# Block products on 12 instead of 8 of the 24 row tiles in the down projections of each FFN's first half

## The chip, the core and the metric

The kernel runs on one core of a Trainium2 chip. The core has five engines that work side by side and wait for each other by semaphores: TensorE (PE in the profile, its weight loads as PEld) multiplies matrices into the accumulators in PSUM; VectorE (DVE) and ScalarE (ACT) work on tiles in SBUF and PSUM; GpSimd (POOL) works on SBUF; SyncE (SP) issues most of the transfers from memory. Each engine takes its instructions in a fixed order. The metric is the device time of one execution in microseconds (us), as the median of a few runs.

## The reference

One decoder layer on 256 tokens of width 2048, all in float32:

```
def swiglu(x, w_gate, w_up, w_down):
    return (jax.nn.silu(x @ w_gate) * (x @ w_up)) @ w_down

x = layer_norm(alpha * x + 0.5 * swiglu(x, ffn1_w_gate, ffn1_w_up, ffn1_w_down), ln1_g, ln1_b)
p = x @ w_in
mix = concatenate([diff_attn_group(p[..., :ATTN_COLS], ...), rwkv7_group(p[..., ATTN_COLS:], ...)]) @ w_out
x = layer_norm(alpha * x + mix, ln2_g, ln2_b)
x = layer_norm(alpha * x + 0.5 * swiglu(x, ffn2_w_gate, ffn2_w_up, ffn2_w_down), ln3_g, ln3_b)
```

The gate and up weights are 2048 x 5632, the down weights 5632 x 2048. The change touches only the two FFNs.

## The kernel before

**Float32 by parts.** Each operand is split into a high part (rounded to a shorter format) and a low part (the rest). A product of a 128-token tile with a row tile of weights (128 x 512) is three matmuls, high by high, high by low and low by high: lines 151, 152 and 153 in `product`. For weights the split is made on the fly: `load` brings a pair of row tiles (a 512 KB transfer, line 131, issued by SP), `halves` makes the high part on ACT (line 141, "wh") and the low part on DVE (line 144, "wl") into one of `NW["ffn"]` = 7 buffer pairs, which are free again once PE has used them. The sections below call such a split pair of row tiles a half.

**Order.** The program is written as one stream and handed to a planner, which lays it out on a simulated time line and by that fixes the order of the instructions on each engine ahead of the run. On the chip each engine follows that order, whatever the real durations are.

**An FFN.** The 5632 hidden columns are done in two halves, of six and of five blocks of 512. For each block j, gate and up are computed over the 16 row tiles of x, then `up_done` makes h = 0.5 silu(gate) up, transposes it on PE, and splits it into tiles hT. After the blocks of a half the down projection runs over that half's h: 24 row tiles in the first half, 20 in the second, 2048 output columns as two calls of `two_blocks`, each with two column blocks of 512. In the first half `down_done` (line 472) loads a piece rc of the residual by ACT's queue, after a one-column copy by GpSimd into the same tile (line 476), and writes alpha times rc plus the accumulator into the SBUF tiles y (line 478). The second half adds into y and ends with the layer norm.

**Block products.** `two_blocks` (from line 206) computes two column blocks for both token tiles together. Over the first eight row tiles, `ks[:8]`, it treats the work as a 2x2 by 2x2 product (two token tiles, two groups of four row tiles, two column blocks) and uses the scheme with seven block products in place of eight. It needs:

- sums of the x (or h) blocks, made once by `combinations` into the tiles S[0] to S[3]: eight sums on DVE (line 379, through temporaries in buffer `y0`), then four cuts into high and low part, the copy on ACT (line 383) and the difference on DVE;
- four raw weight tiles r11, r12, r22, r21 of four row tiles each, out of four buffers of tag `r4`, and four differences of them on DVE in place (`minus`, line 222, 128 x 2048);
- copies and additions of partial accumulators (lines 235 to 255).

`seven` does one block product: two halves of two row tiles each, six matmuls for each half. The remaining row tiles, `ks[8:]`, are plain work: `later` puts them in a list (`tail`), and `late(n)` runs the next n steps of that list, each one half of weights used by both token tiles, 12 matmuls. The rest of the first column block runs in the second half of its own call, the rest of the second column block in the first half of the next call; `n = len(self.tail) // 4` steps stand between one block product and the next, and what is left stands at the end.

**Who waits for whom.** A half must have been loaded (SP and the DMA queues), cast (ACT) and subtracted (DVE) before PE may use it, and its buffer comes free only after PE. Buffers with the names y0 and y1 hold x at the start, then temporaries (`y0`), then y for the rest of the FFN. The S tiles of h replace those of x when the last gate and up block has used them; those of x are stored to memory (`sd`) and read back for the second half.

## Time and profile before

| what | value |
|---|---|
| runs | 1920.59, 1918.80, 1920.53 us (median 1920.53) |
| the profiled execution | 1918.89 us, of which its span 1917.1 us |
| mean granted clock of TensorE | 0.996 of full speed |
| moved by DMA | 381.73 MB, on average 199 GB/s |
| block differences, line 222 | 112, of 2284 ns on average |
| matmuls of block sums, lines 151 to 153 | 448 each |

A row of a waits view reads: engine, tile and line that waited, then what it waited for, then the total in us, the number of times, the longest. A row of a groups view reads: line, engine, operation, output <- inputs, shapes, count, then busy us and the mean of one in ns, then the idle time of the engine in front of them with what ended it. A row of a timeline reads: start, length in us, engine, line, operation, count of instructions merged. The span counts from the first to the last instruction; the time of a run has some 1.8 us around that.

### The profile page before, as it was taken

The page shows a single profiled execution, that of the slowest core. Times are in us where ns is not written, and L with a number is a line of the kernel's source. Part 1 is how long each engine was busy: PE and PEld are TensorE (multiplying, and loading weights), DVE is VectorE, ACT ScalarE, POOL GpSimd, SP SyncE. Part 2 cuts the span into 40 slices and gives each one's busy share as a digit, 9 for nine tenths or more (in the row PEclk, how much of TensorE's full clock was granted, in tenths as well). Part 3 has the DMA queues.
Part 4 walks back from the last instruction along what each step waited for, and adds up shares of the span by engine and source line. Part 5 has one row for each costly group of instructions (what it writes and reads, how often), then busy time and mean ns, then how long its engine had stood idle before and what let it go on. Part 6 is the DMA issues. An engine that isn't in the chain of part 4 may idle for free. (4 is left out here: it accounts for less than half of the span.)

```text
span 1917.1 us, 24935 instructions
## 1 busy us (share of the span) xinstructions
PE 1881.4 (98%) x9335; PEld 1547.7 (81%) x9335; DVE 1623.1 (85%) x1834; ACT 1093.9 (57%) x1376; POOL 74.9 (4%) x110
## 2 busy tenths in 40 slices
PE   8999999999999999999999999999999999999997
PEld 7888888888888878887778877788888888888886
DVE  8999987789999976776678886999999778999986
ACT  6656664566666536645565543566666545666651
POOL 0000101100000000000000000000000110000000
PEclk9999999999999999999999999999999999999999
DMA  9766676765667456555445645775566676566744
GB/s 312 246 201 217 185 239 220 233 212 200 216 213 228 143 172 201 167 159 160 139 132 146 188 135 165 257 255 191 197 214 227 208 245 211 198 205 212 223 159 134
DMA packets 207322, 381.73 MB, mean 199 GB/s; under 512 B 23531, under 2 KB 25649, under 8 KB 206945
## 3 DMA queue, kind: packets, MB, share of 16 engines
q1 hardware_dynamic: 182928, 350.53, 55.7%
q0 software_dynamic: 6832, 15.32, 3.0%
q10 hardware_dynamic: 17440, 14.29, 2.6%
q8 instruction: 73, 1.20, 0.3%
q14 instruction: 49, 0.39, 0.1%
HBM read 368.29 MB, written 11.80 MB: 198 GB/s over the span
## 5 line engine op out<-in xcount | busy, mean ns | idle before, releaser
L141 ACT CAST wh<-raw 128x1024 fp32r<-128x1024 f32 (+2 forms) x833 | 852.6, 1047 | 596.6 <-PE acc L153 365.9
L144 DVE TENSOR_TENSOR wl<-raw,wh 128x1024 fp32r<-128x1024 f32 (+2 forms) x833 | 983.3, 1213 | 207.7 <-ACT wh L141 203.7
L152 PE MATMUL acc<-wl,xh 128*128 128x512 f32 (+1 forms) x1552 | 604.6, 391 | 4.0 <-DVE wl L144 4.0
L153 PE MATMUL acc<-wh,xl 128*128 128x512 f32 (+1 forms) x1552 | 603.2, 390 | 0.5 <-DVE xl L90 0.4
L151 PE MATMUL acc<-wh,xh 128*128 128x512 f32 (+1 forms) x1552 | 597.8, 393 | 5.9 <-ACT xh L89 4.6
L151 PEld LDWEIGHTS acc<-wh,xh 128*128 128x128 f32 x1552 | 291.7, 188 | 69.3 <-ACT xh L89 6.2
L152 PEld LDWEIGHTS acc<-wl,xh 128*128 128x128 f32 x1552 | 292.0, 188 | 63.6 <-DVE wl L144 5.4
L153 PEld LDWEIGHTS acc<-wh,xl 128*128 128x128 f32 x1552 | 292.0, 188 | 61.8 <-DVE xl L90 2.0
L222 DVE TENSOR_TENSOR raw<-raw,raw 128x2048 f32<-128x2048 f32 x112 | 255.8, 2284 | 1.0 <-DMA raw<-in_ffn_w_gate_dram 0.5
L152 PE MATMUL acc<-wl,hh 128*128 128x512 f32 x544 | 212.0, 390 | 0.0
L153 PE MATMUL acc<-wh,hh 128*128 128x512 f32 x544 | 211.4, 389 | 0.0
L151 PE MATMUL acc<-wh,hh 128*128 128x512 f32 x544 | 210.9, 390 | 0.0
L151 PE MATMUL acc<-wh,s 128*128 128x512 f32 x448 | 174.9, 390 | 1.0 <-ACT acc L248 1.0
L153 PE MATMUL acc<-wh,s 128*128 128x512 f32 x448 | 174.6, 390 | 0.0
L152 PE MATMUL acc<-wl,s 128*128 128x512 f32 x448 | 174.4, 389 | 0.0
L151 PEld LDWEIGHTS acc<-wh,hh 128*128 128x128 f32 x544 | 102.1, 188 | 21.7 <-ACT wh L141 0.4
L152 PEld LDWEIGHTS acc<-wl,hh 128*128 128x128 f32 x544 | 102.2, 188 | 21.1
L153 PEld LDWEIGHTS acc<-wh,hh 128*128 128x128 f32 x544 | 102.1, 188 | 20.9
L151 PEld LDWEIGHTS acc<-wh,s 128*128 128x128 f32 x448 | 84.1, 188 | 19.0 <-ACT acc L248 1.5
L153 PEld LDWEIGHTS acc<-wh,s 128*128 128x128 f32 x448 | 84.1, 188 | 17.5
L152 PEld LDWEIGHTS acc<-wl,s 128*128 128x128 f32 x448 | 84.1, 188 | 17.4
L235 ACT COPY acc<-acc 128x512 f32<-128x512 f32 x28 | 16.0, 571 | 51.5 <-PE acc L153 47.7
(264 smaller groups left out, 1100.0 us busy)
## 6 DMA issues: line engine op xcount, KB each, us to landing
raw<-in_ffn_w_up_dram SPq DMA_DIRECT2D x176, 512.0 KB, 5.3
raw<-in_ffn_w_down_dram SPq DMA_DIRECT2D x176, 512.0 KB, 5.4
raw<-in_ffn_w_gate_dram SPq DMA_DIRECT2D x175, 512.0 KB, 4.5
raw<-in_w_in_dram SPq DMA_DIRECT2D x96, 512.0 KB, 3.7
raw<-in_w_out_dram SPq DMA_DIRECT2D x32, 512.0 KB, 4.1
sd<-s POOLq DMA_DIRECT2D x16, 256.0 KB, 4.1
s<-sd POOLq DMA_DIRECT2D x16, 256.0 KB, 5.1
xs<-y ACTq DMA_DIRECT2D x16, 256.0 KB, 3.0
```

The source lines that it names most:

```text
L141: SC.copy(out=wh[:, c, :w], in_=raw[:, c, :w])
L144: self.cut = V.tensor_tensor(out=wl[:, c, :w], in0=raw[:, c, :w], in1=wh[:, c, :w].bitcast(F32), op=ALU.subtract).ins
L151: T.matmul(a, hi, wh[:, j, :w], start=first and j == 0, stop=False, skip_group_check=True)
L152: T.matmul(a, hi, wl[:, j, :w], start=False, stop=False, skip_group_check=True)
L153: i = T.matmul(a, lo, wh[:, j, :w], start=False, stop=last and j == 1, skip_group_check=True)
L222: V.tensor_tensor(out=out, in0=x, in1=y, op=ALU.subtract)
L235: SC.copy(out=u, in_=a)
```

## The change

In the first half of each FFN the down calls use block products for the first 12 row tiles instead of eight, so two groups of six; the remaining 12 are plain. The gate and up blocks and the down calls of the second half keep eight.

- The block sums of h for the two extra row tiles of each group come from h block 2. `half_tiles` makes them after the fourth gate and up block (j = 3): `combinations` on 128 x 256 pieces, with the eight sums on GpSimd (`by=G`), the cuts on ACT and DVE as before, the temporaries in `y0` and the results, S[4] to S[7], in `y1`.
- The extra raw weights (two row tiles each, one transfer of 512 KB) lie in the buffers of the seventh half (wh6, wl6) and in `y0`: `more_raws`. So these calls, and the last gate and up block in front of them, have six buffers for halves (`spare`). The differences are made on both parts, and `seven` runs three halves.
- With y0 and y1 taken, y can't be in SBUF during the first half. `down_done` now computes into rc and stores it to a tile `ys` in memory by ACT's queue; y is read back by GpSimd's queue ahead of the second block of the second half.

```diff
-        def two_blocks(self, cols, ks, x, comb, done, strict=False):
+        def two_blocks(self, cols, ks, x, comb, done, strict=False, extra=None, spare=0):
             assert not self.pend
-            self.buffers(NW["ffn"], LAG["ffn"])
+            self.buffers(NW["ffn"] - spare, LAG["ffn"])
...
-            def own(src, k, c):
-                return self.load(src, row + k, c, n=4)
+            done_rows = 8
+            if extra is not None:
+                done_rows = 12
+                more = dict(zip(("11", "12", "22", "21"), extra()))
+
+            def own(src, k, c, name):
+                r = [self.load(src, row + k, c, n=4)]
+                if extra is not None:
+                    t = more[name]
+                    self.loaded = nc.sync.dma_start(out=t, in_=src[(row + 8 + k // 2) * P:(row + 10 + k // 2) * P, c:c + NB].rearrange("(k p) n -> p k n", p=P)).ins
+                    r.append(t)
+                return r
 
             def minus(out, x, y):
-                V.tensor_tensor(out=out, in0=x, in1=y, op=ALU.subtract)
+                for o, a, b in zip(out, x, y):
+                    V.tensor_tensor(out=o, in0=a, in1=b, op=ALU.subtract)
 
             def seven(acc, lhs, raw, first=False, last=False):
-                for i in range(2):
-                    self.product(acc, lambda j: lhs(2 * i + j), *self.halves(raw[:, 2 * i:2 * i + 2]), first and i == 0, last and i == 1)
+                parts = [raw[0][:, 0:2], raw[0][:, 2:4]] + raw[1:]
+                for i, r in enumerate(parts):
+                    self.product(acc, lambda j: lhs(2 * i + j), *self.halves(r), first and i == 0, last and i + 1 == len(parts))
...
-            self.later(s0, c0, ks[8:], x, (a, w), lambda t, acc: done(0, t, acc), False)
+            self.later(s0, c0, ks[done_rows:], x, (a, w), lambda t, acc: done(0, t, acc), False)
...
-        def combinations(x, tmp, after=None):
-            def add(out, x, y, op=ALU.add):
+        def combinations(x, tmp, after=None, own=None):
+            def add(out, x, y, op=ALU.add, by=V if own is None else G):
                 x, y = (a if a.dtype == F32 else a.bitcast(F32) for a in (x, y))
-                V.tensor_tensor(out=out, in0=x, in1=y, op=op)
+                by.tensor_tensor(out=out, in0=x, in1=y, op=op)
 
             def cut(x, i):
-                hi, lo = s_tiles(i)
+                hi, lo = (own or s_tiles)(i)
                 SC.copy(out=hi, in_=x)
-                add(lo, x, hi, ALU.subtract)
+                add(lo, x, hi, ALU.subtract, V)
...
+        def half_tiles(x):
+            u = fp.tile([P, 8, 2, P], F32R, tag="y1", name=nm("s"))
+            t = fp.tile([P, 4, 2, P], F32, tag="y0", name=nm("xs"))
+
+            def own(i):
+                S[4 + i] = [u[:, 2 * i], u[:, 2 * i + 1]]
+                return S[4 + i]
+
+            combinations({(a, q): [h[:, 2 * q:2 * q + 2] for h in x[(a, 2)]] for a in range(2) for q in range(2)},
+                         [t[:, i] for i in range(4)], None, own)
+
+        def more_raws():
+            r = [fp.tile([P, 2, NB], F32, tag=f"{n}6", name=nm("raw")) for n in ("wh", "wl")]
+            t = fp.tile([P, 4, NB], F32, tag="y0", name=nm("raw"))
+            return r + [t[:, 0:2], t[:, 2:4]]
+
+        ys = [dp.tile([P, D], F32, tag=f"ys{t}", name=nm("ys")) for t in range(2)]
...
-                    stream.two_blocks(((wg, c0), (wu, c0)), KX, x_lhs, comb, lambda i, tt, acc, f=(gate_done, up): f[i](tt, acc), j0 + j == 1)
+                    if half == 1 and j == 1:
+                        y.extend(fp.tile([P, D], F32, tag=f"y{t}", name=nm("y")) for t in range(2))
+                        for t in range(2):
+                            nc.gpsimd.dma_start(out=y[t], in_=ys[t])
+                    stream.two_blocks(((wg, c0), (wu, c0)), KX, x_lhs, comb, lambda i, tt, acc, f=(gate_done, up): f[i](tt, acc), j0 + j == 1,
+                                      spare=int((half, j) == (0, 5)))
+                    if (half, j) == (0, 3):
+                        half_tiles(hT)
...
             combinations(hT, (y_parts, x_parts)[half]())
-            if half == 0:
-                y.extend(fp.tile([P, D], F32, tag=f"y{t}", name=nm("y")) for t in range(2))
...
                     nc.scalar.dma_start(out=rc, in_=res[tt][:, c])
-                    V.scalar_tensor_tensor(out=y[tt][:, c], in0=rc, scalar=ALPHA, in1=acc, op0=ALU.mult, op1=ALU.add)
+                    V.scalar_tensor_tensor(out=rc, in0=rc, scalar=ALPHA, in1=acc, op0=ALU.mult, op1=ALU.add)
+                    nc.scalar.dma_start(out=ys[tt][:, c], in_=rc)
...
-                stream.two_blocks(((wd, n * NB), (wd, (n + 1) * NB)), ks, h_lhs, comb, lambda i, tt, acc, n=n, f=down_done: f(tt, acc, n + i))
+                stream.two_blocks(((wd, n * NB), (wd, (n + 1) * NB)), ks, h_lhs, comb, lambda i, tt, acc, n=n, f=down_done: f(tt, acc, n + i),
+                                  extra=more_raws if half == 0 else None, spare=1 - half)
```

More of the change, by code (lines that the diff above doesn't have):

```diff
@@ L216, in two_blocks @@
             row = ks[0][0]
-            def own(src, k, c):
-                return self.load(src, row + k, c, n=4)
+            done_rows = 8
[9 more added lines that the diff above has]
+                return r
             def minus(out, x, y):
-                V.tensor_tensor(out=out, in0=x, in1=y, op=ALU.subtract)
+                for o, a, b in zip(out, x, y):
+                    V.tensor_tensor(out=o, in0=a, in1=b, op=ALU.subtract)
             def seven(acc, lhs, raw, first=False, last=False):
-                for i in range(2):
-                    self.product(acc, lambda j: lhs(2 * i + j), *self.halves(raw[:, 2 * i:2 * i + 2]), first and i == 0, last and i == 1)
+                parts = [raw[0][:, 0:2], raw[0][:, 2:4]] + raw[1:]
+                for i, r in enumerate(parts):
+                    self.product(acc, lambda j: lhs(2 * i + j), *self.halves(r), first and i == 0, last and i + 1 == len(parts))
             def whole(t, k):
-                return lambda j: x(t, k + j)
+                return lambda j: x(t, k + j if j < 4 else 4 + k // 2 + j)
             n = len(self.tail) // 4
             with tc.issue_after(self.loaded) if strict else ExitStack():
-                r11 = own(s0, 0, c0)
+                r11 = own(s0, 0, c0, "11")
             seven(a, whole(0, 0), r11, True)
@@ L237, in two_blocks @@
             with tc.issue_after(self.loaded) if strict else ExitStack():
-                r12 = own(s1, 0, c1)
+                r12 = own(s1, 0, c1, "12")
             minus(r11, r12, r11)
@@ L244, in two_blocks @@
             with tc.issue_after(self.loaded) if strict else ExitStack():
-                r22 = own(s1, 4, c1)
+                r22 = own(s1, 4, c1, "22")
             minus(r11, r22, r11)
@@ L256, in two_blocks @@
             with tc.issue_after(self.loaded) if strict else ExitStack():
-                r21 = own(s0, 4, c0)
+                r21 = own(s0, 4, c0, "21")
             seven(a, whole(0, 4), r21)
-            self.later(s0, c0, ks[8:], x, (a, w), lambda t, acc: done(0, t, acc), False)
+            self.later(s0, c0, ks[done_rows:], x, (a, w), lambda t, acc: done(0, t, acc), False)
             n = len(self.tail) // 4
@@ L266, in two_blocks @@
             self.late(len(self.tail))
-            self.later(s1, c1, ks[8:], x, (u, v), lambda t, acc: done(1, t, acc), False)
+            self.later(s1, c1, ks[done_rows:], x, (u, v), lambda t, acc: done(1, t, acc), False)
         def flush(self, lag=0):
@@ L405, in comb @@
         def comb(i):
-            return lambda j: (S[i][0][:, j, :], S[i][1][:, j, :])
+            return lambda j: tuple(s[:, j, :] for s in S[i]) if j < 4 else tuple(s[:, j - 4, :] for s in S[4 + i])
         def y_parts():
```

## The prediction

> **What bounds the kernel now.** First the page: span, then busy time of each engine.
>
> ```profile
> span 1917.1 us, 24935 instructions
> ...
> PE 1881.4 (98%) x9335; PEld 1547.7 (81%) x9335; DVE 1623.1 (85%) x1834; ACT 1093.9 (57%) x1376; POOL 74.9 (4%) x110
> ```
>
> TensorE (PE) is busy in all but 35.7 us. Busy PE isn't proof of a bound, so the next view is who PE waited for, over the whole span:
>
> ```profile
> PE acc L151 <- ACT xh L89: 4.6, 5, 1.9
> PE tr L83 <- DMA xc<-in_x_dram: 4.5, 1, 4.5
> PE acc L152 <- DVE wl L144: 4.0, 3, 2.2
> ```
>
> The largest total is 4.6 us, none of it named by a line that the change touches except the 4.0 us behind line 144. Then busy time in four stretches. The first and third run from where VectorE (DVE) passes the third h block of an FFN to where it begins the second down call; the second and fourth are that second call:
>
> ```profile
> 157.00:299.00 142.00, 142.00 (x641) 117.67 (x640) 126.35 (x116) 90.92 (x102) 8.79 (x17) 1.00 0.66 214
> 299.00:361.00 62.00, 62.00 (x275) 51.38 (x274) 47.06 (x41) 31.93 (x33) 9.35 (x12) 1.00 0.76 253
> 1359.00:1501.00 142.00, 142.00 (x640) 117.85 (x639) 126.18 (x110) 88.26 (x100) 1.88 (x2) 1.00 0.64 216
> 1501.00:1563.00 62.00, 62.00 (x275) 51.35 (x274) 45.68 (x39) 31.27 (x33) 7.91 (x12) 1.00 0.76 246
> ```
>
> Columns: length; busy PE, PEld, DVE, ACT, POOL; granted clock; DMA share; GB/s. PE has no gap and the clock is 1.00. DVE is at 89% in the long stretches and 75% in the down call. So each matmul left out is worth its full step, as long as DVE delivers the halves in time. The step:
>
> ```profile
> 257.91 0.39 PE L151 MATMUL acc<-wh,s 128*128 128x512 f32 x1
> 258.13 0.39 PE L152 MATMUL acc<-wl,s 128*128 128x512 f32 x1
> 258.36 0.39 PE L153 MATMUL acc<-wh,s 128*128 128x512 f32 x1
> 258.59 0.39 PE L151 MATMUL acc<-wh,s 128*128 128x512 f32 x1
> ```
>
> Three in 0.68 us: 0.2267 us each (the 0.39 is a pipelined length).
>
> **The gain.** A down call of the first half had 7 block products over 4 row tiles and a plain rest over 16, three matmuls per row tile: 7x4x3 + 2x2x16x3 = 276. Now 7x6x3 + 2x2x12x3 = 270. Six fewer in each of four calls (two per FFN): 24 x 0.2267 = **5.44 us** off PE. This is all that the change can win.
>
> **What DVE gets for it.** Durations by group:
>
> ```profile
> L144 DVE TENSOR_TENSOR wl<-raw,wh 128x1024 fp32r<-128x1024 f32 x823 | 976.0, 1218 | 207.1 <-ACT wh L141 203.0
> L141 ACT CAST wh<-raw 128x1024 fp32r<-128x1024 f32 x823 | 846.1, 1052 | 577.6 <-PE acc L153 354.9 <-DMA raw<-in_ffn_w_down_dram 74.5 <-DVE raw L222 42.7
> ```
>
> Back to back the steps are shorter than the means, since the ends overlap:
>
> ```profile
> 246.63 4.61 DVE L222 TENSOR_TENSOR raw<-raw,raw 128x2048 f32<-128x2048 f32 x2
> 259.19 4.63 DVE L144 TENSOR_TENSOR wl<-raw,wh 128x1024 fp32r<-128x1024 f32 x4 [0.88 <-ACT wh L141]
> 299.09 2.28 DVE L222 TENSOR_TENSOR raw<-raw,raw 128x2048 f32<-128x2048 f32 x1
> 301.29 1.22 DVE L144 TENSOR_TENSOR wl<-raw,wh 128x1024 fp32r<-128x1024 f32 x1
> ```
>
> Line 144 steps by (4.63 - 1.22)/3 = 1.14 us, line 222 by 2.20. A call had 14 + 16 = 30 cut halves and has 21 + 12 = 33; it adds four differences of 128x1024, of the shape of line 144. DVE: 7 x 1.14 = **8.0 us per call**. ACT: 3 x 1.05 = 3.2 us, beside its 30 idle us of 62: nothing.
>
> Behind the fourth gate and up block come four more cuts of 128x256: on ACT at most 4 x 0.62 (the 128x512 row below) = 2.5 us, again in idle time; on DVE 4 x 0.42 by the nearest row (64x256) = 1.7 us.
>
> Both the new sums and the old ones of h use the buffer `y0`, and the new are ahead in the code. So the eight old sums can no longer run early:
>
> ```profile
> 70.00:154.00 84.00, 5.37 (x8) 1.00 0.65 217
> 1265.00:1362.00 97.00, 5.46 (x8) 1.00 0.65 222
> ...
> L383 ACT CAST s<-xs 128x512 fp32r<-128x512 f32 x24 | 14.8, 620 | 4.3 <-DVE xs L379 2.2 <-PE acc L152 1.8
> L902 DVE TENSOR_TENSOR SV<-St,PC 64x256 f32<-64x256 f32 x8 | 3.3, 418 | 0.2
> ```
>
> (Line 379 alone, in two stretches.) I take it that they move behind 157 us: 5.4 us more in the long stretch. The other end is that they stay and the new sums come late; that belongs to the slower case.
>
> Demand on DVE in the first long stretch: 126.35 + 8.0 + 1.7 + 5.4 = 141.5; in FFN 2, 126.18 + 8.0 + 1.7 + 5.5 = 141.4. PE there needs 142 - 6 x 0.2267 = 140.6. **DVE is 0.8 us over.** In the second call 47.06 + 8.0 = 55.1 and 45.68 + 8.0 = 53.7 stand against 60.6: room of 5.5 and 6.9 us.
>
> **What covers an overrun.** The halves wait in seven buffers ahead of PE:
>
> ```profile
> DVE wl L144 <- ACT wh L141: 8.5, 4, 5.2
> ACT wh L141 <- DMA raw<-in_ffn_w_down_dram: 6.6, 3, 5.4
> ACT wh L141 <- POOL rc L476: 3.8, 1, 3.8
> ```
>
> (Waits between 345 and 375 us.) DVE stood idle for 5.2 us while PE ran on without a gap: the cover is at least that. The change takes one buffer of seven in these calls, so I estimate 5.2 x 6/7 = 4.5 us.
>
> **GpSimd's eight sums per FFN** are an operation the trace doesn't have. The nearest rows:
>
> ```profile
> L1054 POOL TENSOR_TENSOR ars<-vr,neghalf 128x4 f32<-128x4 f32 x8 | 8.1, 1014 | 171.4 <-DVE vr L1052 132.8 <-DMA raw<-in_w_in_dram 38.6
> 335.48 0.18 POOL L476 COPY rc<-hh 128x1 f32<-128x1 f32 x1 [9.36 <-DVE y L478]
> 308.24 4.45 POOL L476 COPY rc<-hh 128x1 f32<-128x1 f32 x1 [0.41 <-DVE y L478]
> 370.12 2.18 POOL L476 COPY rc<-hh 128x1 f32<-128x1 f32 x1 [19.98 <-DVE y L478]
> ...
> 308.10 2.28 DVE L222 TENSOR_TENSOR raw<-raw,raw 128x2048 f32<-128x2048 f32 x1
> 310.30 2.35 DVE L144 TENSOR_TENSOR wl<-raw,wh 128x1024 fp32r<-128x1024 f32 x2
> 314.69 2.36 DVE L144 TENSOR_TENSOR wl<-raw,wh 128x1024 fp32r<-128x1024 f32 x2 [2.04 <-ACT wh L141]
> ```
>
> The same one-column copy took 0.18 us, and 4.45 us beside three DVE instructions in a row; it ended at 312.69, when DVE's run ended (312.65). So the two engines shut each other out. How long a sum holds DVE is bounded by 0.18 (the free copy) and 1.01 us (the free sum of four columns); I take the middle, 0.6: 8 x 0.6 = 4.8 us per FFN. Overrun: 0.8 + 4.8 - 4.5 = **1.1 us lost per FFN**, 2.2 in all.
>
> The Trainium skill, "SBUF — State Buffer", section "Who interferes with whom", says that a DVE instruction with two SBUF inputs and a GpSimd instruction that reads SBUF exclude each other for a whole instruction; the trace's 4.45 us agrees for DVE shutting out GpSimd, and no run here shows the reverse. By that rule a sum costs DVE its own length. By the Trainium skill, "GPSIMD Engine Reference", section "3.1 Elementwise — side-by-side cycle accounting", a sum of 2048 columns takes 4497 ns, so 256 columns are an estimated 0.56 us, and the sum would end 0.6 us lower than mine.
>
> **The second call by itself.** Walk it in order, DVE's work minus PE's. A product of three halves: 3 x 1.14 - 18 x 0.2267 = -0.66. One step of the rest: 1.14 - 2.72 = -1.58. A difference with its product: 2.20 + 1.14 - 0.66 = +2.68. The rest has 12/2 = 6 steps, a quarter of which rounds to one (it was two), so: -0.66, -2.24, +0.44, -1.14, +1.54, -0.04, and a difference with an addition (3.34 + 0.6), +3.90; then three steps, -0.8. From low to high 6.1 us against a cover of 4.5: 1.6 us lost if nothing runs ahead; none if differences do, as the pair at 246.63 did. I take 0.4 per FFN: **0.8 us**.
>
> **Edits at no cost.** Transfers: 16 more ACT issues, eight per FFN, and two POOL issues per FFN:
>
> ```profile
> L477 ACTq DMA_DIRECT2D rc<-xs x8: 326/326/359, 1482.5 to 1577.9; - x8
> raw<-in_ffn_w_down_dram SPq DMA_DIRECT2D x176, 512.0 KB, 5.4
> s<-sd POOLq DMA_DIRECT2D x16, 256.0 KB, 5.1
> ```
>
> 8 x 0.33 = 2.6 us of ACT's idle time. Each write of a y quarter makes ACT wait for line 478, with the casts queued behind it; it stands behind at most a 2.28 us instruction on DVE, and ACT was held for 3.8 us by POOL with PE at 62.00 of 62: nothing, 3.8 us at most for all. SP issues 24 transfers of 512 KB per call as before (four more for block products, four fewer for the rest). But the tiles of r22 and r21 wait for `y0`, that is for the last cut of h; SP's later loads stand behind them. r22 is wanted two products after the cuts, about 2 x (4.08 + 2.72) = 13.6 us of PE, against 5.4 us to landing: nothing. With y's 4 MB per FFN written and read back DMA stays below 0.8 of its time. Moving y out of SBUF delays nobody: it is read back ahead of the second half's down calls.
>
> **Sum.** -5.44 + 2.2 + 0.8 = -2.4 us. The profiled execution took 1918.89 us (span 1917.1, 1.8 around it), giving 1916.5. The median of the three runs is 1920.53, 1.6 above it; compared with medians I say 1920.53 - 2.4 = **1918.1 us**.
>
> **Rivals.**
>
> *The cover holds* (0.34): sums hold DVE near 0.2 us each, or fall in its idle moments, or the old sums stay early; 0.8 + 1.6 - 4.5 is below zero. Then the whole 5.4 us: 1915.1. For it: PE had no gap with DVE at 89%, and ACT stood 3.8 us without loss. Against: DVE's demand equals PE's time, which no stretch here shows.
>
> *DVE becomes the bound at the sums* (0.22), the other side. ACT and DVE take work in a fixed order; behind each late sum stands a copy on ACT, behind it the casts, behind them DVE, then PE. With sums of 1.01 us and one hold like the 2.18 us copy per FFN: 0.8 + 8.1 + 2.2 - 4.5 = 6.6 per FFN, 13.2 + 0.8 - 5.4 = +8.6: 1929. It makes the kernel slower by 0.2% (3.8 us; about what a measurement here tells from no change) once holds and waits together pass 0.8 + x - 4.5 = 4.2, x = 7.9 us per FFN: one microsecond per sum.
>
> *My forecast* (0.44): 1916.0 to 1921.5 by itself.
>
> That fewer matmuls don't come out of it can't be: the count is fixed by the loops.
>
> **Chances.** Faster by over 0.2% (below 1916.7): nearly all of the first rival and a little of the forecast, 0.36. Within: 0.43. Slower: 0.21. The range reaches from the full gain less a microsecond of scatter, 1914, to 1927, near the slower case; some 0.18 lies outside.
>
> **What would show it.** Right: line 151 with `s` 480 times instead of 448, all of line 151's FFN and projection matmuls 8 fewer; line 144's halves 12 more; DVE near 98% of the long stretches; PE gaps of one to two microseconds per FFN behind line 144. Wrong towards the gain: no such gaps. Wrong towards slower: ACT's cuts waiting for POOL, POOL's sums of more than 1 us each, PE waits of several microseconds around 160 to 260 and 1360 to 1460 us. Wrong in the step: gaps in the second call only, which the walk priced at 0.4.

## The result and the profile after

The median of the changed kernel is **1942.79 us** (1938.03 to 1944.24, four runs), that of the kernel before 1920.56 us (1918.80 to 1924.70, four runs) on the same chip. The ratio is **1.0108, with a 95% interval of 1.0084 to 1.0133**: the change makes the kernel about 1.1% slower. The forecast was 2.4 us faster, and the time lies above the range. The profiled execution took 1938.03 us, of which the span is 1936.2: 19.1 us more than before.

The page of the kernel after, span and busy time of each engine:

```profile
span 1936.2 us, 25028 instructions
...
PE 1889.3 (98%) x9311; PEld 1551.4 (80%) x9311; DVE 1662.1 (86%) x1870; ACT 1109.4 (57%) x1396; POOL 97.2 (5%) x130
```

PE has 24 matmuls fewer, 9335 - 9311, as it should, and yet its busy time is 7.9 us longer. Fewer matmuls in more busy time means that some took longer; the mean granted clock is 0.990 against 0.996. Who PE waited for, after, over the whole span:

```profile
PE acc L152 <- DVE wl L144: 8.9, 6, 2.2
PE acc L151 <- ACT wh L141: 6.8, 6, 1.8
...
PE acc L151 <- ACT acc L260: 2.3, 4, 0.7
```

Before, the first was 4.0 us in all, the second 0.2, and the third, the copy of an accumulator (then line 248), 1.0. In the stretches of the two FFNs (60 to 440 and 1260 to 1660 us) the list of before is empty: all that stands there after is new. The four stretches of the prediction, after, with the same columns:

```profile
157.00:299.00 142.00, 138.80 (x615) 113.89 (x614) 137.83 (x132) 91.26 (x105) 15.32 (x22) 0.99 0.60 199
299.00:361.00 62.00, 59.30 (x254) 48.33 (x253) 51.42 (x45) 32.21 (x34) 7.81 (x10) 0.97 0.70 237
1369.00:1511.00 142.00, 139.25 (x619) 114.88 (x618) 136.77 (x125) 88.73 (x103) 11.12 (x10) 0.99 0.59 197
1511.00:1573.00 62.00, 58.60 (x250) 47.72 (x249) 52.45 (x46) 32.72 (x34) 10.22 (x9) 0.97 0.68 229
```

Each stretch that had PE busy from end to end now has 2.7 to 3.4 us of gaps, and the granted clock is below 1.00 in all four. (The stretches of FFN 2 are shifted by 10 us, since that FFN starts that much later.)

To see where the time is lost, take a marker that both kernels have: the silu of a gate block, on ACT. Timeline rows of before (line 421): the silu of the second gate block behind the first half of FFN 1, the first silu of FFN 2, and that of the second gate block behind the first half of FFN 2. (At the first gate block behind a half, the silu of the changed kernel stands behind a cast that waited 2.21 us for its load, so that block is no good marker.)

```profile
459.91 0.60 ACT L421 ACTIVATE sg<-acc 128x512 f32<-128x512 f32 x1 [0.26 <-PE acc L153]
...
1236.98 1.09 ACT L421 ACTIVATE sg<-acc 128x512 f32<-128x512 f32 x2
...
1663.61 0.60 ACT L421 ACTIVATE sg<-acc 128x512 f32<-128x512 f32 x1 [0.26 <-PE acc L153]
```

The same three after (line 451):

```profile
467.19 0.60 ACT L451 ACTIVATE sg<-acc 128x512 f32<-128x512 f32 x1 [0.26 <-PE acc L153]
...
1247.53 0.60 ACT L451 ACTIVATE sg<-acc 128x512 f32<-128x512 f32 x1
...
1682.70 0.60 ACT L451 ACTIVATE sg<-acc 128x512 f32<-128x512 f32 x1 [0.26 <-PE acc L153]
```

The kernel after is 7.3 us behind, then 10.6, then 19.1, and 19.1 at the end. So **+7.3 and +8.5 us fall in the first halves of the two FFNs** and +3.3 us between them, in what both kernels do alike; nothing is added behind the last marker. Each first half should have won 2.7 us, so they lose 10.0 and 11.3 us. Three gaps in each make up nearly all of it: 3.8, 4.8 and 1.8 us in FFN 1, and 3.8, 5.5 and 0.9 us in FFN 2, each counted as the time over 0.2267 us for each matmul. The smallest stands at the accumulator copy of line 260 (a wait of 0.66 us in each FFN; in FFN 1 one of 0.44 us for line 141 comes behind it); the other two follow.

### The first gap: behind the fourth gate and up block

The PE timeline of after around 195 us:

```profile
191.59 1.03 PE L459 MATMUL tr<-ident,sg 128*128 128x128 f32 x8
194.72 0.50 PE L152 MATMUL acc<-wl,xh 128*128 128x512 f32 x1 [2.10 <-DVE wl L144]
...
196.86 0.63 PE L151 MATMUL acc<-wh,s 128*128 128x512 f32 x1
...
199.17 0.39 PE L151 MATMUL acc<-wh,s 128*128 128x512 f32 x1
199.40 0.39 PE L152 MATMUL acc<-wl,s 128*128 128x512 f32 x1
```

PE waits 2.10 us for a low part. Then, for some four microseconds, a matmul takes 0.43 us from start to start instead of 0.23. From 194.72 to 199.17 there are 12 steps: 4.45 us instead of 12 x 0.2267 = 2.72. So the gap costs 2.10 + 1.73 = 3.8 us, nearly half of it behind the wait. The windows view of after gives the clock of that stretch and of the like one at 331 us:

```profile
195.00:199.00 4.00, 4.00 (x12) 3.09 (x12) 4.00 (x5) 1.05 (x1) 0.00 (x0) 0.57 1.00 365
...
331.00:335.00 4.00, 3.72 (x10) 2.94 (x11) 4.00 (x4) 2.56 (x4) 0.00 (x0) 0.62 0.36 131
```

Why was the low part late? DVE's work in the 38 us in front of the gap, before:

```profile
157.00:195.00 38.00, 38.00 (x174) 31.54 (x173) 35.54 (x30) 24.64 (x27) 0.00 (x0) 1.00 0.64 214
```

and after:

```profile
157.00:195.00 38.00, 35.90 (x163) 29.66 (x162) 37.81 (x36) 24.41 (x31) 6.02 (x5) 1.00 0.37 121
```

Before there were 2.5 us of room, after there are 0.2. What fills them is seen in the timelines. DVE, after:

```profile
156.38 4.58 DVE L144 TENSOR_TENSOR wl<-raw,wh 128x1024 fp32r<-128x1024 f32 x3 [1.64 <-ACT wh L141]
160.89 0.96 DVE L391 TENSOR_TENSOR s<-xs,s 128x256 fp32r<-128x256 f32 x1
162.03 0.69 DVE L391 TENSOR_TENSOR s<-xs,s 128x256 fp32r<-128x256 f32 x1 [0.19 <-ACT s L395]
162.65 2.83 DVE L233 TENSOR_TENSOR raw<-raw,raw 128x2048 f32<-128x2048 f32 x1
165.40 0.41 DVE L391 TENSOR_TENSOR s<-xs,s 128x256 fp32r<-128x256 f32 x1
...
167.21 2.28 DVE L233 TENSOR_TENSOR raw<-raw,raw 128x2048 f32<-128x2048 f32 x1
...
170.54 1.89 DVE L391 TENSOR_TENSOR xs<-hh 128x512 f32<-128x512 f32 x3
```

and GpSimd, after:

```profile
156.43 1.77 POOL L391 TENSOR_TENSOR xs<-xs 128x256 f32<-128x256 f32 x1
158.28 1.60 POOL L391 TENSOR_TENSOR xs<-hh 128x256 f32<-128x256 f32 x1
```

While GpSimd runs its sums, DVE's instructions are longer: three of line 144 take 4.58 us instead of 3.50, a cut 0.96 and 0.69 instead of 0.41, a difference 2.83 instead of 2.28. That is 1.08 + 0.55 + 0.28 + 0.55 = 2.5 us. The four cuts themselves add 1.6 us. And at 170.54 the old sums of h begin, eight of 0.68 us, which before ran ahead of 154 us: 5.4 us. Together 9.5 us come into a stretch that had 2.5. ACT, which makes the cuts from these sums, waits for GpSimd too, but hardly hands that on: DVE waits 0.19 us for a cut.

### The second gap: in the second down call

DVE, after, at the start of that call:

```profile
303.08 3.50 DVE L144 TENSOR_TENSOR wl<-raw,wh 128x1024 fp32r<-128x1024 f32 x3 [3.49 <-ACT wh L141]
306.61 2.29 DVE L233 TENSOR_TENSOR raw<-raw,raw 128x2048 f32<-128x2048 f32 x1
...
322.44 3.42 DVE L233 TENSOR_TENSOR raw<-raw,raw 128x1024 f32<-128x1024 f32 x2
327.48 3.50 DVE L144 TENSOR_TENSOR wl<-raw,wh 128x1024 fp32r<-128x1024 f32 x3 [1.62 <-ACT wh L141]
```

ACT and GpSimd, after, shortly ahead of the gap, one row of each timeline:

```profile
326.39 1.05 ACT L141 CAST wh<-raw 128x1024 fp32r<-128x1024 f32 x1 [5.76 <-POOL rc L511]
```

```profile
322.35 3.83 POOL L511 COPY rc<-hh 128x1 f32<-128x1 f32 x2 [38.50 <-DMA ys<-rc]
```

PE waits 1.32 and 1.39 us for line 141 around 329 and 331 us, and the clock falls behind them (the 0.62 above): 4.8 us lost against the step, and 5.5 us at the same place in FFN 2. Two causes offer themselves. ACT was held for 5.76 us: it issues the load of rc (line 512), which waits for GpSimd's copy, which waits until rc's store to `ys` has landed and then takes 3.83 us for two copies of one column beside DVE's differences; the casts are queued behind. Or the call as such leaves DVE too little room. The experiments had to tell these apart.

### The profile page after: what moved, and what is told of

The parts are those of the page before. It is cut to its first block, busy times and chain, and to the rows that moved or that the text cites. A ratio compares the mean times of both kernels' runs of the same rounds, so it can differ in the third digit from the quotient of the medians.

```text
span 1936.2 us, 25028 instructions
## 1 busy us (share of the span) xinstructions
PE 1889.3 (98%) x9311; PEld 1551.4 (80%) x9311; DVE 1662.1 (86%) x1870; ACT 1109.4 (57%) x1396; POOL 97.2 (5%) x130
## 5 line engine op out<-in xcount | busy, mean ns | idle before, releaser
L141 ACT CAST wh<-raw 128x1024 fp32r<-128x1024 f32 (+1 forms) x845 | 865.6, 1047 | 596.6 <-PE acc L153 396.4
L144 DVE TENSOR_TENSOR wl<-raw,wh 128x1024 fp32r<-128x1024 f32 (+1 forms) x845 | 999.5, 1217 | 187.3 <-ACT wh L141 182.8
L233 DVE TENSOR_TENSOR raw<-raw,raw 128x2048 f32<-128x2048 f32 (+1 forms) x128 | 276.0, 2161 | 1.4 <-DMA raw<-in_ffn_w_gate_dram 0.5
L152 PE MATMUL acc<-wl,hh 128*128 128x512 f32 x504 | 197.1, 391 | 0.0
L153 PE MATMUL acc<-wh,hh 128*128 128x512 f32 x504 | 196.8, 390 | 0.0
L151 PE MATMUL acc<-wh,hh 128*128 128x512 f32 x504 | 192.1, 391 | 3.1 <-ACT wh L141 3.1
L151 PE MATMUL acc<-wh,s 128*128 128x512 f32 x480 | 189.5, 395 | 5.7 <-ACT wh L141 3.4
L152 PE MATMUL acc<-wl,s 128*128 128x512 f32 x480 | 188.1, 392 | 0.0
L153 PE MATMUL acc<-wh,s 128*128 128x512 f32 x480 | 187.8, 391 | 0.0
L151 PEld LDWEIGHTS acc<-wh,hh 128*128 128x128 f32 x504 | 94.7, 188 | 23.8 <-ACT wh L141 4.3
L151 PEld LDWEIGHTS acc<-wh,s 128*128 128x128 f32 x480 | 91.0, 190 | 27.6 <-ACT wh L141 5.2
L153 PEld LDWEIGHTS acc<-wh,hh 128*128 128x128 f32 x504 | 95.1, 189 | 19.8
L152 PEld LDWEIGHTS acc<-wl,hh 128*128 128x128 f32 x504 | 95.1, 189 | 19.7
L153 PEld LDWEIGHTS acc<-wh,s 128*128 128x128 f32 x480 | 90.8, 189 | 19.1
```

What stands on the lines that cost most here:

```text
L141: SC.copy(out=wh[:, c, :w], in_=raw[:, c, :w])
L144: self.cut = V.tensor_tensor(out=wl[:, c, :w], in0=raw[:, c, :w], in1=wh[:, c, :w].bitcast(F32), op=ALU.subtract).ins
L151: T.matmul(a, hi, wh[:, j, :w], start=first and j == 0, stop=False, skip_group_check=True)
L152: T.matmul(a, hi, wl[:, j, :w], start=False, stop=False, skip_group_check=True)
L153: i = T.matmul(a, lo, wh[:, j, :w], start=False, stop=last and j == 1, skip_group_check=True)
L233: V.tensor_tensor(out=o, in0=a, in1=b, op=ALU.subtract)
```

## The experiments

The kernels of one group ran on the same chip, a different one for each group, beside the kernel before, whose medians were 1920.32 (16 runs), 1920.66 (23) and 1921.36 us (28) in the three groups. "Lost" is counted as above, from the profiled run. Diffs are excerpts; "..." marks what is left out.

### First group: one part at a time

**E1, transfers of rc and ys on GpSimd's queue.**

```diff
-                    nc.scalar.dma_start(out=rc, in_=res[tt][:, c])
+                    nc.gpsimd.dma_start(out=rc, in_=res[tt][:, c])
...
-                    nc.scalar.dma_start(out=ys[tt][:, c], in_=rc)
+                    nc.gpsimd.dma_start(out=ys[tt][:, c], in_=rc)
```

> The changed kernel, with the residual's load and the store of y issued by GpSimd's queue instead of ACT's, so that ACT never waits for the store, GpSimd's copy or VectorE's line that makes y. Theory 'ACT held': the PE gaps in the second down call of each FFN (327 to 331 and 1542 to 1547 us in the changed kernel, 3 waits for ACT's cast there, with a lowered clock behind them, about 4 us each) go, and the kernel takes 7 to 9 us less than the changed one: about 1932 to 1935. Rival 'VectorE overloaded by the third halves': the gaps stay where they are, the time stays within 2 us of the changed kernel.

Measured: 1927.38 us (1922.62 to 1928.79), ratio 1.003 [1.0019, 1.0042]. Most of the loss is gone, more than I had expected of it, but not in the way expected. The profiled span is 10.6 us shorter than that of the changed kernel, and 8.3 us of this lie between the two FFNs, in code that the edit does not touch (see the table below). In the first halves the second gap is smaller and not gone (1.7 us lost in FFN 1, 2.8 in FFN 2), and a new one stands at 410 us. GpSimd's timeline has the row

```profile
324.68 15.04 POOL L511 COPY rc<-hh 128x1 f32<-128x1 f32 x1 [1.79 <-DMA ys<-rc]
```

A copy of one column takes 15.04 us while DVE works without a pause; the loads of rc behind it on the queue come late, and at 410 us line 513 on DVE waits for one. In the profiled run the first gap in FFN 1 also cost only 2.4 us for the same wait of 2.09: there the clock did not fall behind it. So by the profile most of this kernel's gain does not come from the transfers that were moved.

**E2, the new sums on DVE.**

```diff
-            def add(out, x, y, op=ALU.add, by=V if own is None else G):
+            def add(out, x, y, op=ALU.add, by=V):
```

> The changed kernel, with the eight 128x256 sums per FFN on VectorE instead of GpSimd. Theory 'GpSimd shuts VectorE out': VectorE's instructions around 156 to 163 us are back at their usual lengths, and the PE gap at 192 us (2.1 us of waiting for line 144, and a lowered clock behind it) shrinks by the 3 us that they were stretched: 4 to 8 us less in all. Rival 'plain demand': eight sums of 0.42 us each on VectorE cost as much as the stretching (3.4 us against 3.0 us), so the gap stays, and the time is within 2 us of the changed kernel.

Measured: 1938.58 us (1937.57 to 1939.91), ratio 1.0091 [1.0076, 1.0106]. The first gap is gone, though eight sums of 0.42 us are 3.4 us on DVE, not less than the 2.5 by which GpSimd's sums had stretched its work. So the amount alone doesn't explain that gap; part of these sums falls at 156 us, where DVE stood idle for 1.64 us in the changed kernel. The second gap grew (4.9 and 8.0 us lost), so the total fell by only 4.0 us, against the kernels before.

**E3, temporaries of the new sums in a buffer of their own**, so that the old sums of h can run early again.

```diff
-            t = fp.tile([P, 4, 2, P], F32, tag="y0", name=nm("xs"))
+            t = fp.tile([P, 4, 2, P], F32, tag="wh6", name=nm("xs"))
...
-                                      spare=int((half, j) == (0, 5)))
+                                      spare=int((half, j) in ((0, 4), (0, 5))))
```

> The changed kernel, with the temporaries of the new sums in the seventh half buffer in place of y0 (and six buffers from the fifth gate and up block on), so that the eight old sums of h may run early again as before the change. Theory 'moved sums': the 5.4 us of old sums leave the stretch behind 162 us, and the PE gaps at 192 us and 1408 us with their lowered clock go: 7 to 9 us less than the changed kernel. Rival 'the stretch is overloaded anyway': gaps of the same size come, at this or a later place; within 2 us.

Measured: 1936.30 us (1930.34 to 1937.43), ratio 1.0072 [1.0051, 1.0094]. The first gap is gone here too (1.0 us is left); the second lost 3.3 and 7.1 us. So with the old sums early the hold by GpSimd's sums opens no gap of that size, and in E2 the moved sums without that hold opened none either; both together do.

**E4, the kernel before with the change's spill of y to memory, and nothing else.**

```diff
...
-                    V.scalar_tensor_tensor(out=y[tt][:, c], in0=rc, scalar=ALPHA, in1=acc, op0=ALU.mult, op1=ALU.add)
+                    V.scalar_tensor_tensor(out=rc, in0=rc, scalar=ALPHA, in1=acc, op0=ALU.mult, op1=ALU.add)
+                    nc.scalar.dma_start(out=ys[tt][:, c], in_=rc)
```

> The kernel before, with nothing of the change but the way of y: written to memory from rc by ACT's queue, read back ahead of the second block of the second half. No block products on 12 rows, no new sums, seven buffers. Theory 'ACT held': ACT waits 5 us and more for the residual's copy here too; with seven buffers and a lighter VectorE some of it is covered: 0 to 8 us slower than before (1920 to 1929), with PE waits for ACT's cast in the second down call if it is over 2 us. Rival: no PE gap, no difference.

Measured: 1920.26 us (1918.41 to 1925.28), ratio 0.9996 [0.9982, 1.0010], no PE gap in the FFNs. The waits view between 300 and 385 us:

```profile
ACT wh L141 <- POOL rc L480: 8.7, 3, 3.6
```

ACT is held for 8.7 us, and PE loses nothing. The hold alone is not enough to make a gap.

### Second group: is the hold needed at all?

**E5, E1 and E3 together, without GpSimd's copy.** The copy only touched rc; without it GpSimd runs no copy in the down calls that DVE can keep waiting.

```diff
...
-                    G.tensor_copy(out=rc[:, 0:1], in_=hT[(0, 0)][0][:, 0, 0:1].bitcast(F32))
-                    nc.scalar.dma_start(out=rc, in_=res[tt][:, c])
+                    nc.gpsimd.dma_start(out=rc, in_=res[tt][:, c])
...
```

> The changed kernel, with both causes named so far taken away: the temporaries of the new sums in the seventh half buffer (old sums of h early again), and the residual's load and the store of y on GpSimd's queue, without the one-column copy ahead of the load that VectorE kept waiting. Theory 'two stalls': the gaps at 192 and 1408 us and those at 327 and 1542 us are gone; what is left of gaps is 1 us near 278 us in each FFN and 0 to 2 us in the down calls; 1917 to 1922 us. Rival 'VectorE is too full for third halves': gaps of 2 us and more stay in the down calls, 1924 us and more.

Measured: 1929.45 us (1924.67 to 1931.43), ratio 1.0036 [1.0019, 1.0052]. **A miss**: with none of these transfers on ACT, the second gap stayed, 5.2 and 4.3 us lost. The hold isn't necessary either. That speaks for the rival, DVE too full for the third halves.

**E6, E5 with the new sums on DVE** (the edit of E2).

> The kernel of the run before this one (own buffer, GpSimd's queue, no copy), with the new sums on VectorE in place of GpSimd. Theory: with the old sums early there is room for 3.4 us of sums on VectorE as there is for the stretching by GpSimd; within 2 us of that run. Rival 'GpSimd's exclusion still costs': 2 to 6 us less.

Measured: 1924.28 us (1919.11 to 1928.23), ratio 1.0013 [1.0002, 1.0024]: 5.2 us less than E5. In the profiles the first halves are 1.9 and 1.8 us shorter, so the sums on GpSimd still cost time even where they open no gap of two microseconds; a further 3.7 us lie between the FFNs. The second gap is still there (3.9 and 2.8 us lost). Who waited between 296 and 332 us in E6:

```profile
ACT wh L141 <- DMA raw<-in_ffn_w_down_dram: 8.7, 4, 5.4
ACT wh L141 <- DVE raw L233: 7.0, 2, 3.5
...
PE acc L151 <- ACT wh L141: 3.4, 2, 2.0
```

ACT now waits for the first load of the call and then for DVE's differences: the chain is DVE (line 233), ACT, PE.

**E7, the kernel before with six buffers where the change has six.**

```diff
-            self.buffers(NW["ffn"], LAG["ffn"])
+            self.buffers(NW["ffn"] - spare, LAG["ffn"])
...
```

> The kernel before, with six half buffers instead of seven in the last gate and up block and the two down calls of each first half, and nothing else. Theory: the seventh buffer alone carries no load, no PE gap over 1 us, within 2 us of before (1918 to 1922). Rival 'the cover is the buffers': gaps in the down calls, 4 us slower or more.

Measured: 1922.74 us (1921.17 to 1926.41), ratio 1.0014 [1.0004, 1.0023], no PE gap in the FFNs. The buffer is not the cause: the first halves take 0.0 and 0.4 us less than before, and what the profiled execution takes more (4.5 us) lies almost all between the FFNs (4.3 us), where no buffer was taken away.

**E8, the change with block products on eight row tiles.** The new sums are made and not used.

```diff
-                                  extra=more_raws if half == 0 else None, spare=1 - half)
+                                  extra=None, spare=1 - half)
```

> The changed kernel, with eight rows again in the down calls: the new sums are made but not used, y still goes through memory, six buffers. Theory: the gaps at 192 and 1408 us are made by the sums (moved and new) and not by the third halves, so they stay, with 2 us of wait each and a lowered clock behind; the gaps at 327 and 1542 us need the third halves on VectorE together with the held ACT, so they go; 1924 to 1930 us. Rival 'the held ACT and six buffers are enough': gaps there too.

Measured: 1929.58 us (1928.13 to 1930.07), ratio 1.0043 [1.0026, 1.0060]. The only row of PE's waits in each FFN is

```profile
PE acc L152 <- DVE wl L144: 2.1, 1, 2.1
```

So the first gap comes from the sums, since the third halves are absent here and the spill and the six buffers open no gap by themselves (E4, E7). It loses 3.8 us in FFN 1 and, with the same wait but no fall of the clock, 2.2 in FFN 2; the first halves are 3.4 and 2.1 us longer than before. The rest of the 8.9 us by which the median is above the kernel before is not the gap's. The second gap needs the third halves, since it is gone with them.

### Third group: the order of the second call

The steps of the plain rest give DVE room: 12 matmuls on PE for one half. Two lines, `n = len(self.tail) // 4` at 243 and 272, spread them between the block products, `n` at a time. Before there were eight steps and n = 8 // 4 = 2. Now there are six, and n = 6 // 4 = 1; in the first half of a call the other three come in one piece at the end, behind the differences that they should have covered. (The rounding of E10 to E12 acts wherever six steps are left, so in the second half of both calls, too.) With the prediction's steps, a difference with its product and n plain steps takes DVE 2.20 + 1.14 + 3 x 1.14 + n x 1.14 and PE 18 x 0.2267 + n x 2.72. With n = 1 that is 7.9 against 6.8 us, DVE falls behind by 1.1 us each time; with n = 2 it is 9.0 against 9.5, and it catches up.

**E9, block products on 12 row tiles in the first call only** (on E6).

```diff
-                                  extra=more_raws if half == 0 else None, spare=1 - half)
+                                  extra=more_raws if half == 0 and n == 0 else None, spare=1 - half)
```

> The kernel of e6 (new sums on VectorE in a buffer of their own, residual and y on GpSimd's queue without the copy), with block products on 12 rows in the first down call of each first half only; the second call keeps eight, with six buffers. Theory 'the second call's start': VectorE begins that call 5 us late, since its first raw tile can only be loaded when the call before has used the buffer, and then meets the longer differences with no cover left; so the gap at 325 and 1530 us goes with the twelve rows of that call, 12 matmuls (2.7 us) come back, about 1920 us. Rival 'the load of VectorE in both calls': a gap of 2 us or more stays in the first call or moves behind it.

Measured: 1922.09 us (1918.23 to 1925.18), ratio 1.0000 [0.9988, 1.0012]; the second gap is gone; some 0.9 us is lost in each FFN, in FFN 1 at the accumulator copy (line 260). The 12 matmuls saved, 2.7 us, less these 1.9 would be 0.8 us faster, which lies within the interval. The rival's gap in the first call is not there.

**E10, E6 with the steps rounded up.**

```diff
-            n = len(self.tail) // 4
+            n = (len(self.tail) + 3) // 4
...
-            n = len(self.tail) // 4
+            n = (len(self.tail) + 3) // 4
```

> The kernel of e6, with the quarter of the rest rounded up instead of down: of the six plain steps two instead of one stand behind each of the first three block products, as in the kernel before with its eight steps. In the walk of VectorE's work against PE's the largest rise falls from 6.1 to 3.9 us. Theory: the gaps at 325 and 1530 us fall below 1 us and the saved matmuls show: 1915 to 1919 us, faster than before. Rival 'late loads': VectorE isn't what is late there, the gap stays over 2 us, 1922 us and more.

Measured: **1914.27 us** (1912.36 to 1914.88), ratio **0.9961 [0.9949, 0.9973]**: faster than the kernel before by 7.1 us. The second gap is gone in both FFNs, with as many halves and differences as in E6. The second down calls of E10:

```profile
299.00:361.00 62.00, 62.00 (x275) 51.33 (x274) 56.55 (x50) 35.69 (x37) 8.68 (x16) 1.00 0.78 258
...
1501.00:1563.00 62.00, 61.81 (x273) 50.88 (x272) 55.90 (x48) 36.09 (x38) 8.62 (x16) 1.00 0.73 246
```

PE is busy and its clock 1.00 again, while DVE does more in the second call than in the changed kernel (56.55 and 55.90 against 51.42 and 52.45 us) or in E6 (55.16 and 53.67). More work in the same time without a gap: not the amount, the order was at fault. But 7.1 us is more than the 5.4 of the matmuls. The rounding also reaches the second half's calls, whose rest is six steps too; behind the first half of FFN 2, where such calls lie, E10 is 0.15 us shorter than before, so the surplus is not there. The table below shows where it is.

**E11, the change with that rounding alone.**

> The changed kernel, with that rounding alone. Theory: the gaps in the second down call shrink (2.7 and 3.4 us of waiting to under 1.5), those at 192 and 1408 us stay with their lowered clock: 1928 to 1935 us. Rival 'the held ACT makes the gap': it stays as it is, 1938 us and more.

Measured: 1926.29 us (1924.84 to 1927.82), ratio 1.0025 [1.0016, 1.0034], a little better than expected. No second gap, though ACT issues the transfers as in the change; the first gap is there in both FFNs, with its wait of 2.1 us, with 2.4 us lost each (the clock did not fall behind it). The first halves are 6.9 and 6.2 us shorter than in the changed kernel: 10.3 us of these 13.1 are the second gap, about 3 the clock behind the first.

**E12, E10 with ACT's queue and GpSimd's copy as in the change.**

> The kernel of e10, with the residual's load, its copy and the store of y back as in the changed kernel (ACT's queue, GpSimd's copy). Theory 'the held ACT costs only where VectorE has no room': with the rounding it costs 0 to 3 us over e10. Rival 'it is a cause by itself': the gap behind the wait of 5.8 us comes back, 4 us and more over e10.

Measured: 1918.83 us (1915.42 to 1923.42), ratio 0.9985 [0.9977, 0.9993]. Against E10 in the same group the held ACT costs 4.6 us, more than the 0 to 3 that I had expected. In the profiles E12's first halves are 0.8 and 4.8 us longer than E10's. It is not one gap that comes back, as the rival said, but several small ones, all in FFN 2. PE's longest waits there:

```profile
PE acc L152 <- DVE wl L144: 1.9, 4, 0.7
PE acc L151 <- ACT wh L141: 1.4, 2, 1.2
```

### The sum of it

The first column is the median against the kernel before of the same group, in us. The others compare the profiled execution with that of the kernel before: its span, the first halves of the FFNs and what lies between them, bounded by the silu rows used above (what is missing to the span, up to 2.2 us, lies ahead of the first silu).

| kernel | median | span | first half, FFN 1 | first half, FFN 2 | between |
|---|---|---|---|---|---|
| the change | +22.2 | +19.1 | +7.6 | +8.5 | +3.3 |
| E11: steps rounded up | +4.9 | +6.4 | +0.7 | +2.3 | +2.2 |
| E12: and sums on DVE, with their own buffer | -2.5 | -2.1 | -0.6 | +4.5 | -6.4 |
| E10: and rc and ys on GpSimd's queue, no copy | -7.1 | -5.0 | -1.4 | -0.3 | -4.8 |
| E1: the change, rc and ys on GpSimd's queue | +7.1 | +8.5 | +6.2 | +5.5 | -5.0 |
| E4: before, spill only | -0.1 | +3.0 | -0.5 | 0.0 | +2.9 |

The stretch between is the same code in all of them but for the rounded steps, and E1, E10 and E12 are 5.0 to 6.4 us shorter there. In these three the planner laid out another order: when VectorE's some 820 instructions there are aligned with those of another kernel, at most 22 find no partner among these three, and at least 44 between one of the three and any other kernel. Waits of PE near the end of that stretch go with it, before (1165 to 1195 us):

```profile
PE acc L151 <- ACT xh L89: 1.9, 1, 1.9
PE acc L151 <- DVE y L1114: 0.9, 1, 0.9
```

and in E10, in the same window:

```profile
PE acc L151 <- ACT xh L89: 0.4, 1, 0.4
```

That the order shortens the stretch is not shown by an experiment of its own. It is more than the scatter that the profiles show: E4 has the order of the kernel before there, on VectorE and ScalarE, and took 2.9 us longer.

So the steps from row to row mean different things. The change to E11, -17.3 us, is the second gap in the main. E11 to E12, -7.5, is **not** the first gap: the first halves give -1.3 and +2.2 us, the stretch between -8.5. E12 to E10, -4.6, is the held ACT, in FFN 2. And that E10 ends ahead of the kernel before is for the most part the stretch between; its first halves are 1.4 and 0.3 us shorter, where 2.7 each were to be won. The steps depend on their order, too: taken last, the rounding is worth 10.7 us (E6 to E10), of which the profiles have 5.6 in the first halves and 3.4 between.

## Why the prediction was wrong

**The count was right.** By-form groups of after:

```profile
L144 DVE TENSOR_TENSOR wl<-raw,wh 128x1024 fp32r<-128x1024 f32 x835 | 992.2, 1222 | 186.5 <-ACT wh L141 182.1
...
L151 PE MATMUL acc<-wh,hh 128*128 128x512 f32 x504 | 192.1, 391 | 3.1 <-ACT wh L141 3.1
L151 PE MATMUL acc<-wh,s 128*128 128x512 f32 x480 | 189.5, 395 | 5.7 <-ACT wh L141 3.4 <-ACT acc L260 2.3
...
L391 POOL TENSOR_TENSOR xs<-xs 128x256 f32<-128x256 f32 x8 | 10.0, 1247 | 0.6
...
L395 ACT CAST s<-xs 128x256 fp32r<-128x256 f32 x8 | 3.2, 404 | 6.3 <-POOL xs L391 6.3
```

Line 151 has 480 matmuls with `s` and 40 fewer with `hh`, eight fewer in all; line 144 has 12 halves more. That each matmul left out is worth its full step is not shown: in E10, the best run, the first halves are 1.4 and 0.3 us shorter than before, not 2.7. In FFN 1 some 0.9 us of what is missing stands at the accumulator copy (line 260, a wait of 0.66 us), for which the prediction had no term; the changed kernel has that wait in both FFNs.

**The step that failed by most is the walk of the second call**, which the prediction put at 0.4 us per FFN. It saw that n falls from two to one and found 6.1 us from low to high, then set a cover of 4.5 us against it. Measured: 4.8 and 5.5 us lost, 10.3 in place of 0.8, and both gone with the order as the only edit (E11). The cover was the error. It was read from one idle spell of 5.2 us. DVE's timeline of before, that spell and the one at the start of the second down call:

```profile
294.54 4.63 DVE L144 TENSOR_TENSOR wl<-raw,wh 128x1024 fp32r<-128x1024 f32 x4 [4.38 <-ACT wh L141]
...
357.01 4.63 DVE L144 TENSOR_TENSOR wl<-raw,wh 128x1024 fp32r<-128x1024 f32 x4 [5.21 <-ACT wh L141]
```

Each is DVE waiting, through ACT, for the first loads of a call: at 293 us ACT had waited 4.55 us for that transfer. Such a spell does show that PE lives through it; but it comes back at the start of each call (3.49 us in the kernel after, at 303 us), and so, as I read it, the lead of the halves is spent when the walk begins; no view shows the lead itself. The prediction set the cover against the sums and again against the walk, and in the walk it is gone.

**The sums.** That the old sums of h move, and by 5.4 us, was right, and so were DVE's additions. The excess was then averaged over 142 us: 0.8 over and 4.8 for GpSimd, against a cover of 4.5. The trace has the excess in the first 38 us: 9.5 us into 2.5 us of room, 7.0 over; less the same 4.5 that is 2.5, and PE waited 2.10. So this term, 2.2 us for both FFNs, came out at 7.6 (3.8 us twice). The hold was 2.5 us in the rows above, not 4.8, so a term too large stood beside a stretch too long. A sum on GpSimd took 1.25 us on average in the form `xs<-xs`, where the prediction took 0.6 as what it holds DVE for. The Trainium skill, "GPSIMD Engine Reference", section "3.1 Elementwise — side-by-side cycle accounting", has 4497 ns for a sum of 2048 columns, an estimated 0.56 us for 256; beside a busy DVE the row above has more than twice that, and the row decides.

**The clock was not in the sum at all.** A wait of 2.1 us was priced at 2.1 and cost 3.8. At the four large gaps of the two FFNs that is 7 to 8 us that no term held. It is partly chance: behind the same wait in E11 the clock did not fall.

**The held ACT** was priced at nothing, 3.8 us at most. By itself that is right (E4, 8.7 us of hold without loss). Beside the fuller DVE it costs 4.6 us (E12 against E10), a little above the upper end.

**The rivals.** "DVE becomes the bound at the sums", 1929 us, had the place of the first gap and the right sign. Its chain over ACT did not carry it: by the last row above ACT's cuts waited 6.3 us for GpSimd in all, but DVE hardly waited for them; GpSimd held DVE directly. Its price for the sums, 13.2 us, is above the 6.0 us lost at the first gaps of E8 and the 7.6 of the changed kernel; what takes the time on to 1942.79 is the second call, which it left at 0.8. "The cover holds" is refuted for this kernel. That E10 comes out at 1914.27 us, near that rival's 1915.1, is luck: most of it was won between the FFNs.

What stays open: why the profiled run lies 4.8 us below the median of its kernel (the clock's fall behind some gaps and not behind others would do part of it, but only one execution has a profile), the 3.3 us that are lost between the first halves of the two FFNs (E4, with the order of the kernel before, lost 2.9 there), why sums on DVE close the first gap, and why the planner's order between the FFNs is a better one in E1, E10 and E12.

## What to carry to other kernels

Room on an engine counts only where it lies: make the sum of demand against time for the shortest stretch between two points at which the lead is used up, and don't use an idle spell as cover in a place where the same spell recurs. When a change moves work from plain steps to block steps, look at how the loop spreads the plain ones: here integer division put half of them where they hid nothing, and rounding up alone took away 17.3 of 22.2 us of loss (E11). A gap on TensorE of about two microseconds is to be priced at once to nearly twice its length. And where a planner lays out the program, an edit can move the order of code that it does not touch: compare the profiles stretch by stretch before a gain is put down to the edit.

## What the runs showed of the hardware

**The clock can fall behind a short gap.** A wait of 2.10 us, 3.1 us from the start of the last transposes to the next matmul, was followed by some four microseconds at a step of 0.427 us in place of 0.227 and a granted clock of 0.57. The Trainium skill, "TensorE: Matmul & The Clock Gate", section "Part 1: The HAM clock gate", says that the clock halves after at least one idle window of about 3.4 us, and that the window runs freely, so that the moment varies. The half step agrees. The wait that sets it off is shorter here than the page's window, and the two waits of 1.32 and 1.39 us at 329 us, with a single matmul recorded between them, did it too. Of the eight waits of 2.1 us at this place in the changed kernel, E1, E8 and E11, four are followed by it (granted clock 0.57 to 0.64 in the next four microseconds) and four are not (1.00). That would fit a window that runs freely; no run here shows the window itself.

**DVE and GpSimd hold each other up, and a busy DVE can keep GpSimd out over many instructions.** The Trainium skill, "SBUF — State Buffer", section "Who interferes with whom", says that a DVE instruction with two inputs in SBUF contends with a GpSimd instruction that reads SBUF, by an exclusive lock on the ports that they share. Both directions are in these traces: DVE's instructions grew by some 0.3 to 0.55 us beside each of GpSimd's sums, and in E1 a one-column copy by GpSimd took 15.04 us, up to the 339.7 us at which a run of two-input DVE instructions in SBUF ended with one that reads an accumulator.
